# A softmax that streams from HBM: tiles of twelve rows in four slots, with an inner loop over groups of four, in place of tiles of eight in six slots

## The chip, the cores and the metric

The kernel runs on one core of one Trainium2 chip. The metric is the device time of one execution in microseconds (us); less is better. Times of before are those of nine runs, and one more execution was recorded by the hardware profiler.

## The reference

`x` has 32 x 512 rows of 1024 float32 numbers; `temperature` is 0.5. Each row gets a softmax of its own:

```python
scaled = x / temperature
shifted = scaled - np.max(scaled, axis=-1, keepdims=True)
exp_x = np.exp(shifted)
return exp_x / np.sum(exp_x, axis=-1, keepdims=True)
```

So 67.1 MB are read and 67.1 MB written. Nothing is shared between rows.

## The kernel before

The 16384 rows are cut into 16 tiles. A tile is 1024 rows: each of the 128 partitions holds 8 rows that follow each other in memory, 32 KB per partition, 4 MB per tile. The tile lies in one of six slots of the buffer `ring` (line 38); everything is done in place, and a slot goes from load to computation to store and then to the load of the tile six further on.

Each engine runs its own program, and semaphores set the order:

- **SyncE (SP)** issues all loads in order (lines 67 to 70). From tile 6 on it waits before each until the store that used the slot has landed (line 69). Last of all it issues the store of the last tile (lines 126 and 127) and waits for all stores.
- **TensorE** only turns "loaded" of each slot into a count, `ready` (line 72).
- **VectorE (DVE)** loops over the tiles (line 80). It waits for `ready` (line 82). Then, for three groups of 4, 2 and 2 rows: the maximum of each row (line 84), a wait for that result, and -2 times the maximum as a bias (line 91). Then, for the same groups: a wait until ScalarE has the sums, the reciprocal (line 96), a wait for it, and one multiplication per row (line 102). The helper `take` (line 63) waits for a semaphore and takes the count off again.
- **ScalarE (ACT)** loops over the tiles (line 109), and for each of the 8 rows computes exp(2x + bias) and its sum in one activation (line 115); ahead of rows 0, 4 and 6 it waits for the bias of that group.
- **GpSimd (POOL)** issues the stores of all tiles but the last, in order (lines 75 to 78). It waits once for the third load, and then before each store until VectorE has scaled the tile (line 77).

The groups are written out in Python, so VectorE's and ScalarE's programs hold one tile's instructions, and only the loop over tiles turns on the chip. Within it a row's place in `ring` is worked out in registers from the tile's number.

Of the kernel before, what the change touches and what calls it, by code (L numbers as in the profile page):

```python
# [1 line left out]

# [4 lines left out]

SLOTS, ROWS = 6, 8  # L10

GROUPS = [4, 2, 2]


@with_exitstack
def kernel(
    ctx: ExitStack,
    tc: tile.TileContext,
    x: bass.AP,
    temperature: bass.AP,  # L20
    out: bass.AP,
):
    nc = tc.nc
    f32 = mybir.dt.float32
    scale = 1.0 / float(temperature)
    extreme = mybir.AluOpType.max if scale > 0 else mybir.AluOpType.min

    P = 128
    xf = x.flatten_outer_dims()
    of = out.flatten_outer_dims()  # L30
    n, d = xf.shape
    tiles = n // (P * ROWS)
    assert tiles * P * ROWS == n and sum(GROUPS) == ROWS
    groups = [(sum(GROUPS[:g]), k) for g, k in enumerate(GROUPS)]
    of_group = dict(groups)

    pool = ctx.enter_context(tc.tile_pool(name="data", bufs=1))
    ring = pool.tile([P, SLOTS * ROWS, d], f32, name="ring")
    top = pool.tile([P, ROWS], f32, name="top")
    bias = pool.tile([P, ROWS], f32, name="bias")  # L40
    sums = pool.tile([P, ROWS], f32, name="sums")
    recip = pool.tile([P, ROWS], f32, name="recip")
    warm = pool.tile([P, 1], f32, name="warm")

    loaded = [tc.alloc_semaphore(f"loaded{s}") for s in range(SLOTS)]
    stored = [tc.alloc_semaphore(f"stored{s}") for s in range(SLOTS)]
    ready, topped, biased, summed, inverted, scaled, finished = (
        tc.alloc_semaphore(name)  # L50
        for name in ("ready", "topped", "biased", "summed", "inverted", "scaled", "finished")
    )

    def dram(t, i):
        return t[P * ROWS * i : P * ROWS * (i + 1), :].rearrange("(p k) d -> p k d", p=P, k=ROWS)

    def slot(i):
        s = i % SLOTS
        return ring[:, ROWS * s : ROWS * (s + 1), :]

    def take(engine, sem, count=1):

        engine.wait_ge(sem, count).then_inc(sem, -count)  # L63

    with tc.tile_critical(no_gpsimd_drain=True):  # L65

        for i in range(tiles):
            if i >= SLOTS:
                nc.sync.wait_ge(stored[i % SLOTS], 16 * (i // SLOTS))
            nc.sync.dma_start(out=slot(i), in_=dram(xf, i)).then_inc(loaded[i % SLOTS], 16)  # L70
        for i in range(tiles):
            nc.tensor.wait_ge(loaded[i % SLOTS], 16 * (i // SLOTS + 1)).then_inc(ready, 1)


        nc.gpsimd.wait_ge(loaded[2], 16)
        for i in range(tiles - 1):
            nc.gpsimd.wait_ge(scaled, len(groups) * (i + 1))
            nc.gpsimd.dma_start(out=dram(of, i), in_=slot(i)).then_inc(stored[i % SLOTS], 16)  # L78

        with nc.vector.Fori(0, tiles) as t:  # L80
            first = t % SLOTS * ROWS
            take(nc.vector, ready)
            for a, k in groups:
                nc.vector.tensor_reduce(  # L84
                    out=top[:, a : a + k],
                    in_=ring[:, bass.ds(first + a, k), :],
                    axis=mybir.AxisListType.X,
                    op=extreme,
                ).then_inc(topped, 1)
                take(nc.vector, topped)  # L90
                nc.vector.tensor_scalar_mul(  # L91
                    bias[:, a : a + k], in0=top[:, a : a + k], scalar1=-scale
                ).then_inc(biased, k)
            for a, k in groups:
                take(nc.vector, summed, k)
                nc.vector.reciprocal(  # L96
                    recip[:, a : a + k], sums[:, a : a + k]
                ).then_inc(inverted, 1)
                take(nc.vector, inverted)
                for b in range(a, a + k):  # L100
                    row = ring[:, bass.ds(first + b, 1), :]
                    ins = nc.vector.tensor_scalar_mul(row, in0=row, scalar1=recip[:, b : b + 1])  # L102
                ins.then_inc(scaled, 1)


        nc.scalar.activation(  # L106
            warm, nc.const_aps.tensor(0.0, (P, 1)), mybir.ActivationFunctionType.Exp
        )
        with nc.scalar.Fori(0, tiles) as t:
            first = t % SLOTS * ROWS  # L110
            for b in range(ROWS):
                row = ring[:, bass.ds(first + b, 1), :]
                if b in of_group:
                    take(nc.scalar, biased, of_group[b])
                nc.scalar.activation(  # L115
                    row,
                    row,
                    mybir.ActivationFunctionType.Exp,
                    bias=bias[:, b : b + 1],
                    scale=scale,  # L120
                    accum_out=sums[:, b : b + 1],
                ).then_inc(summed, 1)


        i = tiles - 1
        nc.sync.wait_ge(scaled, len(groups) * tiles)
        nc.sync.dma_start(out=dram(of, i), in_=slot(i)).then_inc(finished, 16)
        for i in range(tiles - SLOTS, tiles - 1):
            nc.sync.wait_ge(stored[i % SLOTS], 16 * (i // SLOTS + 1))
    with tc.tile_critical(no_gpsimd_drain=True):  # L130
        nc.sync.wait_ge(finished, 16, synchronizes=[nc.sync.lower_ap(slot(tiles - 1))])


# [1 line left out]
_INS = ['x', 'temperature']  # L135
_OUTS = [((32, 512, 1024), 'float32')]

_NUMBERS = {'temperature': 0.5}


# [26 lines left out]
```

## Time and profile before

| | |
|---|---|
| median of 9 runs | 318.43 us (318.25 to 319.11) |
| the profiled execution | 318.38 us, its span 316.6 us |
| VectorE busy | 244.4 us, 77% |
| ScalarE busy | 148.1 us, 47% |
| GpSimd busy | 8.3 us, 3% |
| bytes read, written | 67.11 MB, 67.11 MB: 424 GB/s over the span |
| reduce of 4 rows, of 2 rows (line 84) | 4416 ns, 2286 ns |
| multiplication of a row (line 102) | 749 ns |
| reciprocal of 4 values, of 2 (line 96) | 178 ns, 157 ns |
| activation of a row (line 115) | 1135 ns, 128 of them |
| loads (line 70), median from issue to landing | 49.4 us |
| stores (line 78), the same | 43.7 us |
| last store (line 127) | 17.2 us |

The span runs from the first to the last instruction of the profiled execution. Busy time leaves out what an engine's sequencer does for itself: register operations, branches and semaphores. In rows of tenths, each digit is the busy share of one fortieth of the span. A line of a timeline has the start, the duration, engine, source line, operation, what it writes and reads; in brackets is the idle time ahead of it and what ended it. DVEq and ACTq are the sequencers of VectorE and ScalarE, SPq that of SyncE.

### The profile page before, as it was taken

To read this page: it belongs to the slowest core of one execution; us is meant where nothing else is said; L and a number is where in the kernel's file an instruction comes from. 1 tells how busy PE (TensorE), PEld (TensorE's weight loads), DVE (VectorE), ACT (ScalarE), POOL (GpSimd) and SP (SyncE) were. 2 spreads that over 40 slices of the span, in tenths; PEclk is the share of its full clock that TensorE was granted. 3 is DMA by queue.
4 is the path that set the end of the run, shared out by engine and by line. 5 is a ranking of instruction groups with operands and counts; after the bars stand their busy time and mean duration, and the time that the engine had idled before them with its cause. 6 is when DMAs were issued, how large, how long until landed. Compare 5 with 4: busy or idle time off the path is not lost. (4 is left out here: it accounts for less than half of the span.)

```text
span 316.6 us, 1208 instructions
## 1 busy us (share of the span) xinstructions
DVE 244.4 (77%) x272; ACT 148.1 (47%) x258; POOL 8.3 (3%) x19
## 2 busy tenths in 40 slices
DVE  0299999999999999996959969597795978959600
ACT  1065655556464747380824709156190652907300
POOL 0000000000000000000000000000000000000000
DMA  8999999999999999999999999999999999999995
GB/s 319 410 460 402 397 455 406 464 397 464 402 460 418 443 439 422 447 414 455 406 460 402 460 418 447 422 439 443 418 451 410 460 397 464 402 460 418 443 431 236
DMA packets 4608, 134.22 MB, mean 424 GB/s; under 512 B 512, under 2 KB 512, under 8 KB 512
## 3 DMA queue, kind: packets, MB, share of 16 engines
q1 hardware_dynamic: 2448, 71.30, 52.6%
q0 software_dynamic: 2160, 62.92, 46.0%
HBM read 67.11 MB, written 67.11 MB: 424 GB/s over the span
## 5 line engine op out<-in xcount | busy, mean ns | idle before, releaser
L115 ACT ACTIVATE ring<-ring,bias x128 | 145.1, 1135 | 147.0 <-ACTq L63 147.0
L84 DVE TENSOR_REDUCE top<-ring 128x2 f32 (+1 forms) x48 | 143.8, 2996 | 39.3 <-DVEq L63 39.3
L102 DVE TENSOR_SCALAR ring<-ring,recip x128 | 89.1, 749 | 7.2 <-DVEq L63 1.5
L115 ACT ACTIVATION_READ_ACCUMULATOR ring<-ring,bias 128x1 f32 x128 | 24.0, 187 | 0.0
L78 POOL DMA_DIRECT2D out_dram<-ring x15 | 8.1, 542 | 270.9 <-DVE ring L102 238.4
L91 DVE TENSOR_SCALAR bias<-top 128x2 f32<-128x2 f32 (+1 forms) x48 | 8.2, 170 | 7.2
L96 DVE RECIPROCAL recip<-sums 128x2 f32<-128x2 f32 (+1 forms) x48 | 7.9, 164 | 0.0
L106 ACT ACT_TABLE_LOAD x1 | 1.3, 1283 | 0.9 <-SPq L65 0.9
L106 ACT ACTIVATE warm<-const-float32-0.0 128x1 f32<-128x1 f32 x1 | 0.2, 203 | 0.0
L148 POOL MEMSET const-float32-0.0<- 128x1 f32 x1 | 0.1, 99 | 0.2 <-issue 0.2
L148 POOL MEMSET const-bfloat16-1.0<- 128x1 bf16 x1 | 0.1, 103 | 0.0
L148 POOL MEMSET const-float32-1.0<- 128x1 f32 x1 | 0.1, 99 | 0.0
L148 POOL MEMSET const-uint8-127<- 128x1 uint8 x1 | 0.1, 99 | 0.0
## 6 DMA issues: line engine op xcount, KB each, us to landing
ring<-in_x_dram SPq DMA_DIRECT2D x16, 4096.0 KB, 49.4
out_dram<-ring POOLq DMA_DIRECT2D x15, 4096.0 KB, 43.7
out_dram<-ring SPq DMA_DIRECT2D x1, 4096.0 KB, 17.2
```

Of the source, the lines that this page charges most:

```text
L78: nc.gpsimd.dma_start(out=dram(of, i), in_=slot(i)).then_inc(stored[i % SLOTS], 16)
L84: nc.vector.tensor_reduce(out=top[:, a : a + k], in_=ring[:, bass.ds(first + a, k), :], axis=mybir.AxisListType.X, op=extreme,).then_inc(t ...
L91: nc.vector.tensor_scalar_mul(bias[:, a : a + k], in0=top[:, a : a + k], scalar1=-scale).then_inc(biased, k)
L96: nc.vector.reciprocal(recip[:, a : a + k], sums[:, a : a + k]).then_inc(inverted, 1)
L102: ins = nc.vector.tensor_scalar_mul(row, in0=row, scalar1=recip[:, b : b + 1])
L106: nc.scalar.activation(warm, nc.const_aps.tensor(0.0, (P, 1)), mybir.ActivationFunctionType.Exp)
L115: nc.scalar.activation(row, row, mybir.ActivationFunctionType.Exp, bias=bias[:, b : b + 1], scale=scale, accum_out=sums[:, b : b + 1],).th ...
L148: nc = _bacc.Bacc("TRN2", target_bir_lowering=False, num_devices=1)
```

## The change

There are now ten tiles of twelve rows per partition (6 MB each) and a last one of eight, in four slots of twelve rows: the buffer has 48 rows per partition, as before. All groups have four rows, three in a tile and two in the last. VectorE and ScalarE no longer have the groups written out: an inner loop on the chip turns once per group, with a count that is worked out from the tile's number, so that it turns twice in the last tile. Rows, bias, sums and reciprocals are now addressed through registers that hold the group's number. The counts on the semaphores follow: one per group in place of one per row on `biased` and `summed`. The order of loads and stores, the engines that issue them and the gate on the third load are as they were.

```diff
-SLOTS, ROWS = 6, 8
+TILES = [12] * 10 + [8]
+SLOTS = 4
 
-GROUPS = [4, 2, 2]
+GROUP = 4
...
+    groups = [k // GROUP for k in TILES]
...
+    ring = pool.tile([P, SLOTS * most, d], f32, name="ring")
...
+        rows = t[P * sum(TILES[:i]) : P * sum(TILES[: i + 1]), :]
+        return rows.rearrange("(p k) d -> p k d", p=P, k=TILES[i])
...
+    def loop_groups(engine, t):
+
+        if groups[-1] == groups[0]:
+            return engine.Fori(0, groups[0])
+        short = t // (tiles - 1) * (groups[0] - groups[-1])
+        return engine.Fori(0, groups[0] - short)
...
         with nc.vector.Fori(0, tiles) as t:
-            first = t % SLOTS * ROWS
+            first = t % SLOTS * most
             take(nc.vector, ready)
-            for a, k in groups:
+            with loop_groups(nc.vector, t) as g:
+                group = bass.ds(g * GROUP, GROUP)
                 nc.vector.tensor_reduce(
-                    out=top[:, a : a + k],
-                    in_=ring[:, bass.ds(first + a, k), :],
+                    out=top[:, group],
+                    in_=ring[:, bass.ds(first + g * GROUP, GROUP), :],
...
-                ).then_inc(biased, k)
-            for a, k in groups:
-                take(nc.vector, summed, k)
...
+                ).then_inc(biased, 1)
+            with loop_groups(nc.vector, t) as g:
+                group = bass.ds(g * GROUP, GROUP)
+                take(nc.vector, summed)
+                nc.vector.reciprocal(recip[:, group], sums[:, group]).then_inc(inverted, 1)
                 take(nc.vector, inverted)
-                for b in range(a, a + k):
-                    row = ring[:, bass.ds(first + b, 1), :]
-                    ins = nc.vector.tensor_scalar_mul(row, in0=row, scalar1=recip[:, b : b + 1])
+                for b in range(GROUP):
+                    row = ring[:, bass.ds(first + g * GROUP + b, 1), :]
+                    ins = nc.vector.tensor_scalar_mul(
+                        row, in0=row, scalar1=recip[:, bass.ds(g * GROUP + b, 1)]
+                    )
                 ins.then_inc(scaled, 1)
...
-            for b in range(ROWS):
-                row = ring[:, bass.ds(first + b, 1), :]
-                if b in of_group:
-                    take(nc.scalar, biased, of_group[b])
-                nc.scalar.activation(
...
+            with loop_groups(nc.scalar, t) as g:
+                take(nc.scalar, biased)
+                for b in range(GROUP):
+                    row = ring[:, bass.ds(first + g * GROUP + b, 1), :]
+                    column = bass.ds(g * GROUP + b, 1)
+                    ins = nc.scalar.activation(
...
+                ins.then_inc(summed, 1)
```

More of the change, by code (lines that the diff above doesn't have):

```diff
@@ L31 @@
     n, d = xf.shape
[L32 to L35, printed above, removed]
+    tiles, most = len(TILES), max(TILES)
+    assert sum(TILES) * P == n and all(k % GROUP == 0 for k in TILES)
+    groups = [k // GROUP for k in TILES]
+    assert all(g == groups[0] for g in groups[:-1]) and groups[-1] <= groups[0]
     pool = ctx.enter_context(tc.tile_pool(name="data", bufs=1))
[L38 to L42, printed above, removed]
+    ring = pool.tile([P, SLOTS * most, d], f32, name="ring")
+    top = pool.tile([P, most], f32, name="top")
+    bias = pool.tile([P, most], f32, name="bias")
+    sums = pool.tile([P, most], f32, name="sums")
+    recip = pool.tile([P, most], f32, name="recip")
     warm = pool.tile([P, 1], f32, name="warm")
@@ L54, in dram @@
     def dram(t, i):
-        return t[P * ROWS * i : P * ROWS * (i + 1), :].rearrange("(p k) d -> p k d", p=P, k=ROWS)
+        rows = t[P * sum(TILES[:i]) : P * sum(TILES[: i + 1]), :]
+        return rows.rearrange("(p k) d -> p k d", p=P, k=TILES[i])
     def slot(i):
-        s = i % SLOTS
-        return ring[:, ROWS * s : ROWS * (s + 1), :]
+        first = most * (i % SLOTS)
+        return ring[:, first : first + TILES[i], :]
     def take(engine, sem, count=1):
         engine.wait_ge(sem, count).then_inc(sem, -count)
+    def loop_groups(engine, t):
[3 more added lines that the diff above has]
+        return engine.Fori(0, groups[0] - short)
     with tc.tile_critical(no_gpsimd_drain=True):
@@ L76 @@
         for i in range(tiles - 1):
-            nc.gpsimd.wait_ge(scaled, len(groups) * (i + 1))
+            nc.gpsimd.wait_ge(scaled, sum(groups[: i + 1]))
             nc.gpsimd.dma_start(out=dram(of, i), in_=slot(i)).then_inc(stored[i % SLOTS], 16)
         with nc.vector.Fori(0, tiles) as t:
-            first = t % SLOTS * ROWS
+            first = t % SLOTS * most
             take(nc.vector, ready)
-            for a, k in groups:
+            with loop_groups(nc.vector, t) as g:
+                group = bass.ds(g * GROUP, GROUP)
                 nc.vector.tensor_reduce(
-                    out=top[:, a : a + k],
-                    in_=ring[:, bass.ds(first + a, k), :],
+                    out=top[:, group],
+                    in_=ring[:, bass.ds(first + g * GROUP, GROUP), :],
                     axis=mybir.AxisListType.X,
@@ L91 @@
                 nc.vector.tensor_scalar_mul(
-                    bias[:, a : a + k], in0=top[:, a : a + k], scalar1=-scale
-                ).then_inc(biased, k)
-            for a, k in groups:
-                take(nc.vector, summed, k)
-                nc.vector.reciprocal(
-                    recip[:, a : a + k], sums[:, a : a + k]
-                ).then_inc(inverted, 1)
-                take(nc.vector, inverted)
-                for b in range(a, a + k):
-                    row = ring[:, bass.ds(first + b, 1), :]
-                    ins = nc.vector.tensor_scalar_mul(row, in0=row, scalar1=recip[:, b : b + 1])
+                    bias[:, group], in0=top[:, group], scalar1=-scale
+                ).then_inc(biased, 1)
[3 more added lines that the diff above has]
+                nc.vector.reciprocal(recip[:, group], sums[:, group]).then_inc(inverted, 1)
+                take(nc.vector, inverted)
+                for b in range(GROUP):
[3 more added lines that the diff above has]
+                    )
                 ins.then_inc(scaled, 1)
@@ L109 @@
         with nc.scalar.Fori(0, tiles) as t:
-            first = t % SLOTS * ROWS
-            for b in range(ROWS):
-                row = ring[:, bass.ds(first + b, 1), :]
-                if b in of_group:
-                    take(nc.scalar, biased, of_group[b])
-                nc.scalar.activation(
[L116 to L122, printed above, removed]
+            first = t % SLOTS * most
+            with loop_groups(nc.scalar, t) as g:
[4 more added lines that the diff above has]
+                    ins = nc.scalar.activation(
+                        row,
+                        row,
+                        mybir.ActivationFunctionType.Exp,
+                        bias=bias[:, column],
+                        scale=scale,
+                        accum_out=sums[:, column],
+                    )
+                ins.then_inc(summed, 1)
         i = tiles - 1
-        nc.sync.wait_ge(scaled, len(groups) * tiles)
+        nc.sync.wait_ge(scaled, sum(groups))
         nc.sync.dma_start(out=dram(of, i), in_=slot(i)).then_inc(finished, 16)
```

## The prediction

> **What bounds the kernel now.** I read the page's busy rows first, then the table of stretches, then the store issues in order of time, then one stretch of VectorE.
>
> The page's rows of busy time (tenths in 40 slices):
>
> ```profile
> DVE 244.4 (77%) x272; ACT 148.1 (47%) x258; POOL 8.3 (3%) x19
> ...
> DVE  0299999999999999996959969597795978959600
> ...
> DMA  8999999999999999999999999999999999999995
> ...
> q1 hardware_dynamic: 2448, 71.30, 52.6%
> q0 software_dynamic: 2160, 62.92, 46.0%
> ```
>
> The table of stretches (us; DVE, ACT, POOL busy; clock; DMA share; GB/s):
>
> ```profile
> 33.00:126.00 93.00, 87.61 (x102) 54.98 (x96) 3.33 (x6) 1.00 1.01 431
> 126.00:280.00 154.00, 123.11 (x137) 73.31 (x128) 4.80 (x9) 1.00 1.00 433
> 280.00:298.00 18.00, 15.23 (x17) 9.16 (x16) 0.00 (x0) 1.00 1.00 433
> 298.00:312.80 14.80, 0.08 (x1) 0.00 (x0) 0.00 (x0) 1.00 0.99 430
> 312.80:316.60 3.80, 0.00 (x0) 0.00 (x0) 0.00 (x0) 1.00 0.02 9
> ```
>
> The 16 DMA engines are full from about 2 us to about 313 us: the two queues take 98.6% of 316.6, or 312.2 us. The bytes are the bound. There are 4608 packets, of which 512 are under 512 B; the other 4096 are one 32 KB run per partition and transfer, 256 on each engine. The packet records give 1.21 us each, whether loads run alone, stores alone, or both in turn, one packet from each queue. So a 4 MB transfer is 8 rounds, 9.7 us alone and 19.4 us beside the other queue.
>
> The store issues, start and duration (us):
>
> ```profile
> 110.79 0.53 POOL L78 DMA_DIRECT2D out_dram<-ring  x1 [15.58 <-DVE ring L102]
> 126.90 0.53 POOL L78 DMA_DIRECT2D out_dram<-ring  x1 [15.58 <-DVE ring L102]
> 143.44 0.53 POOL L78 DMA_DIRECT2D out_dram<-ring  x1 [16.01 <-DVE ring L102]
> 162.82 0.53 POOL L78 DMA_DIRECT2D out_dram<-ring  x1 [18.85 <-DVE ring L102]
> 182.17 0.53 POOL L78 DMA_DIRECT2D out_dram<-ring  x1 [18.81 <-DVE ring L102]
> ```
>
> Until about 127 us a tile leaves every 16.1 us: VectorE works off the tiles loaded at the start at its own speed. Then every 19.4 us, because VectorE has caught up and takes each tile as it lands. So VectorE has 3.3 us to spare per tile of 8 rows, and it is the one engine that could become the bound.
>
> VectorE in its compute-bound stretch, one tile's start and part of its end:
>
> ```profile
> 110.41 4.41 DVE L84 TENSOR_REDUCE top<-ring 128x4 f32 x1
> 114.97 0.17 DVE L91 TENSOR_SCALAR bias<-top 128x4 f32<-128x4 f32 x1
> 115.11 2.29 DVE L84 TENSOR_REDUCE top<-ring 128x2 f32 x1
> ...
> 120.27 0.18 DVE L96 RECIPROCAL recip<-sums 128x4 f32<-128x4 f32 x1
> 120.59 2.74 DVE L102 TENSOR_SCALAR ring<-ring,recip  x4
> 123.25 0.15 DVE L96 RECIPROCAL recip<-sums 128x2 f32<-128x2 f32 x1
> ```
>
> A group of four costs 115.11 - 110.41 = 4.70 us to reduce and 123.25 - 120.27 = 2.98 us to scale.
>
> **The change, part by part.**
>
> *Bytes.* 134.22 MB before and after. With 12 rows a partition's run is 48 KB, so I take a packet as 1.5 x 1.21 = 1.815 us. No row shows a 48 KB packet. The price per packet and transfer has a lower end: a 4 B semaphore packet took 9 ns, so if each data packet carries so much besides its bytes, 256 - 176 = 80 fewer packets an engine, and 10 fewer semaphore packets (32 transfers become 22), save at most 90 x 9 ns = 0.8 us. The upper end is every 48 KB run split in two: 10 x 2 transfers x 16 + 16 = 336 packets an engine, 80 more than now, +0.7 us. I take -0.4 us, the half of the first, since a long run has shown no reason to be split.
>
> The Trainium skill (DMA: Bandwidth & Descriptors, "Anatomy of one DMA") puts about 2.0 us of fixed cost on each DMA, so by it ten fewer would save 20 us if each were paid in turn. The trace disagrees: the first three loads ended at 12.98, 22.66 and 32.34 us, 9.68 us apart, which is eight packets and no gap; the fixed part is a latency that the next transfer covers. The same page ("Where 436 GB/s comes from") gives a ceiling of 435.2 GB/s; 134.22 MB at that takes 308.4 us, an estimate that leaves at most 3.8 us to save of 312.2.
>
> *VectorE, per tile of 12.* In the before form it would be 3 x 4.70 + 3 x 2.98 = 23.0 us. The inner loops add register and branch instructions. The built program has, between one bias and the next reduce, a register operation, a move, a subtraction, the branch and two register operations; before has one register operation. The sequencer's records at the outer loop's turn before give prices: addition at 93.13, branch 93.20, move 93.39, semaphore 93.48, long register operation 93.57 (125 ns; short ones 69). So about 0.07, 0.19, 0.09, 0.10 and 0.2 us between starts. Between bias and reduce: 0.07 + 0.07 + 0.07 + 0.19 + 0.2 + 0.1 = 0.7 against 0.1 us, and an addition ahead of the bias 0.07: about +0.68 us a group, exposed, since the reduce cannot be issued earlier: 3 x 0.68 = 2.0 us. In the scale loop the long register operation stands between reciprocal and first multiply: +0.14 us a group, 0.4 us; the rest is issued while four multiplies (2.74 us) run. Leaving the first loop for the second costs +0.2. Sum: 23.0 + 2.6 = **25.7 us** (from 23.0, all hidden, to 26.9, the additions half as long again). Per tile the DMA needs 16 x 1.815 = 29.0 us, so VectorE stays ahead in the middle.
>
> *ScalarE.* 12 rows x 1.13 = 13.6 us, beginning about 5 us into a tile; its loop turns hide under a running activation (before, the first turn's addition, branch and move stood at 23.98 to 24.20, under the activation from 23.25 to 24.38). Its third group ends near 20.3 us, the scale loop wants it at 22.7. Nothing.
>
> *Last tile, two groups of four.* Reduces 2 x 5.38 = 10.8; the second bias releases ScalarE at about 10.2, four rows end at 14.9; scale ends at 15.0 + 3.2 = 18.2 us. Before: 281.87 to 298.08, 16.2 us.
>
> *The schedule.* The first reduce before came at 13.70 = 4.0 + 9.7; after, 4.0 + 14.5 = 18.5. The store gate (third load) before at 4.0 + 29.0 = 33.0, as the trace has it; after at 4.0 + 43.6 = 47.6, which costs nothing, since four loads (58 us of DMA) are queued: the engines only read longer and write later. Load 3 and store 0 then share, store 0 ends near 76.7, and load 4 starts. Store 1 is issued at 18.5 + 2 x 25.7 = 69.9; the first store before took 4.25 us from issue to first packet, so 74.2, in time with 2 us to spare. From there a load lands every 29.0 us: load 4 at 107.5, load 9 at 252.7, and load 10 (8 rounds of 1.815 + 1.21 us) at 276.9. VectorE: 18.5 + 9 x 25.7 = 249.8, so it has caught up and starts tile 9 at 253.1, tile 10 at 278.8, ending at 297.0. Before, the last data packets ended at 313.7 (one engine 314.8), and the last store needs 9.7 us alone: its packets must be there by 304, so its issue by about 301 (before it took 3.4 us from issue to first packet). **Slack: 4 us.** The floor holds.
>
> *Sum against the profiled execution.* 318.38 us was measured with a span of 316.6 (1.8 around it); 318.38 - 0.4 = **318.0**. The median of the runs, 318.43, is 0.05 above that execution: no difference.
>
> **The rivals.**
>
> *A, the floor holds (0.65).* 317.4 to 318.6, around 318.0. For it: share 1.00 in every stretch, and 4 us of slack at the only place where the queues can run dry.
>
> *B, VectorE becomes the bound (0.20): slower.* The chain is first landing + ten tiles + the last: 18.5 + 10c + 18.2 must stay under 301, so c under 26.4 us. That is 0.7 us over my 25.7, or 0.23 us a group, a quarter of what I priced from other instructions. Beyond it every 0.1 us of c, paid by ten tiles, costs 1 us, and the DMA engines stand idle ahead of the last two stores. At c = 26.9 it is 18.5 + 269 + 18.8 + 3.4 + 9.7 = 319.4 of data end against 313.7, about 324 us. Against it: the branch and moves have rows in this trace.
>
> *C, a gap at a hand-over, or a slower long packet (0.08): slower.* Four slots hold the same 48 rows but hand back in larger pieces; where store 0 ends at 76.7 and store 1 is late, or the two ends stand dry, 1 to 2 us are lost, and a split run costs up to 0.7: 319 to 320.5.
>
> *D, the packet saving is larger (0.07).* One engine ends 1.1 us after the others before, its store packets being a little longer (1.23 to 1.25 us); a third fewer may take that too: 0.8 + 0.4, 317.2.
>
> **How the numbers follow.** This measurement can tell about 0.2%, 0.64 us, from no change: faster is under 317.8, slower over 319.1. Of A's 0.65 I give 0.17 to faster, 0.43 to within, 0.05 to slower; B is slower; of C 0.06 slower and 0.02 within; D is faster. Together 0.24 faster, 0.45 within, 0.31 slower. Forecast 318.0. The range reaches from D, 317.2, to where B has used over half of its chance, 322.5; for the likeliest case alone 317.4 to 318.6.
>
> **What would show it.** DMA share 1.00 from 2 to 313 us; 3168 packets; reduce to reduce 5.4 us, reciprocal to reciprocal 3.1 us, a tile 25.7 us in the early stretch; first reduce at 18.5, first store issue at 47.6; last reduce starting near 279 and the last store issued near 297; store issues 29 us apart late. Wrong if a tile takes over 26.4 us, if the DMA row falls under 9 anywhere before the last slice, or if 48 KB packets are not 1.5 times 32 KB ones.

## The result, and the profile after

The changed kernel takes 319.56 us (median of 9 runs, 319.19 to 319.99) against 318.43 us: ratio 1.0033, 95% interval 1.0025 to 1.0042. It is slower by 1.1 us. The forecast was 318.0, a little faster than before. The profiled execution took 319.65 us with a span of 317.8.

The page of the changed kernel, rows of busy time and queues:

```profile
DVE 237.6 (75%) x224; ACT 149.9 (47%) x258; POOL 5.7 (2%) x14
...
DVE  0057898788879879878887887978887877798600
...
DMA  7999999999999999999999999999999999999994
...
DMA packets 3168, 134.22 MB, mean 422 GB/s; under 512 B 352, under 2 KB 352, under 8 KB 352
...
q1 hardware_dynamic: 1728, 71.30, 52.5%
q0 software_dynamic: 1440, 62.92, 45.8%
```

The DMA engines are as full as before and the packets are the 3168 that were counted: no 48 KB run was split. Only the ends differ: 7 in place of 8 at the start, 4 in place of 5 at the end. The table of stretches of the changed kernel, and then the same two last stretches of the kernel before:

```profile
126.00:280.00 154.00, 128.88 (x121) 83.46 (x144) 2.67 (x5) 1.00 1.00 432
280.00:298.00 18.00, 15.35 (x15) 8.16 (x15) 0.53 (x1) 1.00 0.99 429
298.00:313.00 15.00, 2.92 (x5) 1.11 (x2) 0.00 (x0) 1.00 1.00 426
313.00:317.80 4.80, 0.00 (x0) 0.00 (x0) 0.00 (x0) 1.00 0.08 34
```

```profile
298.00:313.00 15.00, 0.08 (x1) 0.00 (x0) 0.00 (x0) 1.00 0.98 424
313.00:316.60 3.60, 0.00 (x0) 0.00 (x0) 0.00 (x0) 1.00 0.02 9
```

The new time is in the last row. After 313 us the kernel before has a share of 0.02 in 3.60 us; the changed one has 0.08 in 4.80 us, which is 6 us of one DMA engine (0.08 x 4.80 x 16): a few engines still work when the others are done. The row above it reads 1.00 all the same: a mean over 16 engines hides the last one.

VectorE in a tile of the changed kernel (start, duration):

```profile
77.62 4.42 DVE L95 TENSOR_REDUCE top<-ring  x1 [0.73 <-issue]
82.28 0.17 DVE L102 TENSOR_SCALAR bias<-top  x1 [0.23 <-DVEq L66]
83.17 4.42 DVE L95 TENSOR_REDUCE top<-ring  x1 [0.72 <-issue]
...
88.58 0.18 DVE L108 RECIPROCAL recip<-sums  x1 [0.60 <-DVEq L66]
89.18 2.74 DVE L112 TENSOR_SCALAR ring<-ring,recip  x4 [0.41 <-DVEq L66]
91.83 0.17 DVE L108 RECIPROCAL recip<-sums  x1
```

Reduce to reduce is 83.17 - 77.62 = 5.55 us (4.70 before), reciprocal to reciprocal 91.83 - 88.58 = 3.25 (2.98). The bracket "issue" is time in which the engine waited for nothing that the profile shows; the records of VectorE's sequencer put its register operations and the branch there. A tile can be read from the store issues:

```profile
203.62 0.53 POOL L88 DMA_DIRECT2D out_dram<-ring  x1 [25.70 <-DVE ring L112]
229.85 0.53 POOL L88 DMA_DIRECT2D out_dram<-ring  x1 [25.70 <-DVE ring L112]
256.11 0.53 POOL L88 DMA_DIRECT2D out_dram<-ring  x1 [25.72 <-DVE ring L112]
284.06 0.53 POOL L88 DMA_DIRECT2D out_dram<-ring  x1 [27.42 <-DVE ring L112]
```

The first three are 26.23 and 26.26 us apart, against the DMA's 29.0. VectorE catches up with the loads only for tile 9, whose load lands from 254.18 (first DMA engine) to 256.7 (last). The start of that tile, and then the last store, by SyncE, of the changed kernel and of the kernel before:

```profile
257.42 4.42 DVE L95 TENSOR_REDUCE top<-ring  x1 [1.61 <-DVEq L66]
302.74 0.35 SPq L141 DMA_DIRECT2D out_dram<-ring  x1
```

```profile
298.11 0.35 SPq L127 DMA_DIRECT2D out_dram<-ring  x1
```

Where the 1.2 us between the two traces come from shows in the landings. Each transfer raises its semaphore once per DMA engine, so the trace has 16 landing times for each. This table is worked out from them, for all kernels of this study. Its columns: how far the 16 are apart in the second load transfer; how far the last is behind the first in a store transfer late in the run (the last whose first landing is before 295 us, but one that still has other work behind it); and the first and last landing of the last store.

```
kernel                     median us  ratio    load 1   store near 290  last store
before                     318.43     -        0.59     1.52            313.69  315.31
after                      319.56     1.0033   1.52     2.88            313.69  316.55
e1  loops, 8 rows          327.62     1.0287   0.42     1.97            324.33  324.49
e2  written out, 12 rows   319.52     1.0030   1.28     1.63            313.46  315.17
e3  12 rows, 16 KB         320.88     1.0073   1.01     2.65            315.01  317.90
e4  12 rows, stores by SP  321.09     1.0076   1.70     5.35            313.46  318.78
e5  12 rows as 8 + 4       319.69     1.0044   0.80     2.34            314.03  316.60
e6  the same, 48 KB apart  320.16     1.0059   0.88     2.58            314.12  316.93
e7  8 rows, 96 KB apart    318.48     1.0002   0.68     1.75            313.69  315.53
e8  8 rows, 16 KB          319.78     1.0045   0.44     1.48            315.15  316.79
e9  after, first load cut  318.90     1.0019   1.18     2.51            313.84  316.10
e10 e2, first load cut     318.43     1.0009   1.05     2.10            313.37  315.57
e11 8 rows, long start     318.61     1.0006   0.48     2.17            313.52  315.71
e12 e2 again               318.29     1.0003   1.15     1.93            313.28  315.20
e13 after again            319.54     1.0030   0.87     2.82            313.64  316.52
e14 e2 again, beside e13   319.04     1.0026   0.89     2.46            313.55  315.98
e15 last tile written out  318.87     1.0019   0.86     2.10            313.34  315.58
e16 e2, last store late    319.83     1.0036   1.55     3.25            314.67  316.85
e17 before, last store late 318.60    1.0008   0.60     1.48            313.73  315.35
e18 before, still later    321.52     1.0087   0.68     1.34            318.28  318.43
```

The landings are those of the traced execution. In e2 it was the fastest of the runs (318.27 us) and in e4 the slowest (321.85); in the others it lies within 0.3 us of the median.

Before and after, the first DMA engine ends at 313.69 in both. The last one ends at 315.31 and 316.55. The difference of the two traces is in how far the last engine is behind the first, and it was 1.36 us further behind already near 290 us, before the last store was issued. The engines between them are later too: the mean of the 16 landings of the last store is 313.96 before and 314.33 after.

### The profile page after: what moved, and what is told of

Its sections match the earlier page's. It is cut to its first block, busy times and chain, and to the rows that moved or that the text cites. A ratio compares the mean times of both kernels' runs of the same rounds, so it can differ in the third digit from the quotient of the medians.

```text
span 317.8 us, 1878 instructions
## 1 busy us (share of the span) xinstructions
DVE 237.6 (75%) x224; ACT 149.9 (47%) x258; POOL 5.7 (2%) x14
## 2 busy tenths in 40 slices
DMA packets 3168, 134.22 MB, mean 422 GB/s; under 512 B 352, under 2 KB 352, under 8 KB 352
## 5 line engine op out<-in xcount | busy, mean ns | idle before, releaser
L95 DVE TENSOR_REDUCE top<-ring x32 | 141.3, 4417 | 36.4 <-DVEq L66 21.2
L112 DVE TENSOR_SCALAR ring<-ring,recip x128 | 87.7, 749 | 13.2 <-DVEq L66 13.2
L128 ACT ACTIVATION_READ_ACCUMULATOR ring<-ring,bias x128 | 23.9, 187 | 0.0
L108 DVE RECIPROCAL recip<-sums x32 | 5.5, 173 | 8.0 <-DVEq L66 8.0
L102 DVE TENSOR_SCALAR bias<-top x32 | 5.5, 171 | 7.4 <-DVEq L66 7.4
L88 POOL DMA_DIRECT2D out_dram<-ring x10 | 5.5, 546 | 278.7 <-DVE ring L112 230.9
## 6 DMA issues: line engine op xcount, KB each, us to landing
ring<-in_x_dram SPq DMA_DIRECT2D x10, 6144.0 KB, 36.6
```

Of the source, the lines that this page charges most:

```text
L95: nc.vector.tensor_reduce(out=top[:, group], in_=ring[:, bass.ds(first + g * GROUP, GROUP), :], axis=mybir.AxisListType.X, op=extreme,).th ...
L102: nc.vector.tensor_scalar_mul(bias[:, group], in0=top[:, group], scalar1=-scale).then_inc(biased, 1)
L108: nc.vector.reciprocal(recip[:, group], sums[:, group]).then_inc(inverted, 1)
L128: ins = nc.scalar.activation(row, row, mybir.ActivationFunctionType.Exp, bias=bias[:, column], scale=scale, accum_out=sums[:, column],)
```

## The experiments

Each edit is against the kernel named. Theories changed on the way; each expectation says which it weighs. Single traces are one execution each, while the medians are of 5 to 12 runs.

**e1: inner loops over groups of four, at tiles of eight.** The changed kernel with the tiles and slots of before:

```diff
-TILES = [12] * 10 + [8]
-SLOTS = 4
+TILES = [8] * 16
+SLOTS = 6
```

> Inner loops alone: sixteen tiles of eight rows in six slots, as before, with the inner loops over groups of four. Theory skew (what ends last is one DMA engine that runs behind the others, and the long packets put it further behind; VectorE is not the bound): packets are those of before, so 318.4 us, ratio 0.999 to 1.001. Theory VectorE (the loops make a tile long, the last store is issued late, and DMA engines run dry ahead of it): the loops add 2 x 0.85 + 2 x 0.25 us to a tile of 8 rows, less one group's own costs, so a last store about 1.5 to 2 us later than 298.1, and some of it in the time: 318.8 to 320.

Measured: 327.62 us, 1.0287 (1.0273 to 1.0301). Both expectations were far too low. The stretches near the end and two store issues:

```profile
296.00:306.00 10.00, 8.20 (x6) 5.50 (x9) 0.00 (x0) 1.00 0.98 419
306.00:314.00 8.00, 5.36 (x9) 3.77 (x8) 0.00 (x0) 1.00 0.00 0
314.00:325.80 11.80, 0.00 (x0) 0.00 (x0) 0.00 (x0) 1.00 0.83 355
```

```profile
276.22 0.53 POOL L88 DMA_DIRECT2D out_dram<-ring  x1 [18.20 <-DVE ring L112]
294.94 0.53 POOL L88 DMA_DIRECT2D out_dram<-ring  x1 [18.19 <-DVE ring L112]
```

A tile takes 18.72 us on VectorE, so sixteen end at 13.75 + 16 x 18.72 = 313.3, where the last store is issued; from 306 to 314 the DMA share is 0.00. This is the rival in which VectorE becomes the bound, at tiles of eight. With two groups of four, VectorE also waits 1.6 us in each tile for ScalarE's second group. The last tile of e2 (below), eight rows in two groups of four without a loop, has the same wait. One line of e1, then three of e2:

```profile
310.04 0.18 DVE L108 RECIPROCAL recip<-sums  x1 [1.59 <-DVEq L66]
```

```profile
280.19 4.42 DVE L95 TENSOR_REDUCE top<-ring 128x4 f32<-128x4096 f32 x1 [1.03 <-DVEq L66]
294.47 0.18 DVE L108 RECIPROCAL recip<-sums 128x4 f32<-128x4 f32 x1 [1.57 <-DVEq L66]
297.57 0.35 SPq L147 DMA_DIRECT2D out_dram<-ring  x1
```

That tile lasts 17.4 us, against 16.2 for the last tile of the kernel before with its groups of 4, 2 and 2. So about half of the 2.6 us that a tile is longer in e1 belongs to the groups of four, not to the loops, and no run has the loops with the old groups. The groups alone would, by an estimate, not have made the last store late: 281.87, where the last tile began before, and 17.4 give 299.3.

In the tiles of twelve rows that wait is gone and a row costs 26.23 / 12 = 2.19 us in place of 18.72 / 8 = 2.34. So the two halves of the change are not two small things: the loops over groups of four cost 9.1 us at tiles of eight, and the larger tiles hide nearly all of it.

**e2, e12, e14: larger tiles alone.** The changed kernel, groups of four included, with the groups written out in Python, for VectorE and ScalarE, the last tile behind the loop:

```diff
-            with loop_groups(nc.vector, t) as g:
+            for g in range(n):
...
+        with nc.vector.Fori(0, tiles - 1) as t:
+            vector_tile(t, groups[0])
+        vector_tile(tiles - 1, groups[-1])
```

> Tiles alone: ten tiles of twelve rows and one of eight in four slots, the groups of four written out, so that a tile takes about 23.1 us on VectorE in place of 26.2. Theory skew: 319.3 to 319.8 us, as the changed kernel, ratio 1.003. Theory VectorE: last store issued some 5 us earlier than 302.7, and the time back at 318.0 to 318.5.

> The kernel with twelve rows and groups written out, once more for a second trace: its first one was of its fastest run. Theory first packet: 319.4 us, loads land 1.3 to 1.7 us apart at the start and the last engine ends that and a drift of about 1 us behind. Theory drift: the loads start as in the first trace and the lag grows by more than 1.5 us.

> The same tiles with the groups written out, on the same chip: last store issued near 297.7 us. Theory late store (what the loops cost is that the last store comes when the DMA engines have no other packets, so that its first packet is not covered by one before it): 0.5 to 0.9 us under the changed kernel. Theory spread (the difference lies in how far apart the DMA engines start and drift, which the engines' loops do not touch): the same as the changed kernel within 0.2 us.

Measured: 319.52 (1.0017 to 1.0042), 318.29 (0.9993 to 1.0013) and 319.04 (1.0013 to 1.0039), on three occasions, each on another chip, and from 317.96 to 320.81 between runs. The last store is issued near 298 us each time. So the larger tiles alone cost nothing on one occasion and up to 1.0 us on another. Their first engine ends at 313.28 to 313.55, 0.1 to 0.4 us before that of the kernel before. That fits the saving of the packets that the prediction put at 0.4; the last engine's lag takes it back.

**e3, e8: the length of packets.** All transfers in pieces of four rows, 16 KB packets; e3 from the changed kernel, e8 from the kernel before:

```diff
-            nc.sync.dma_start(out=slot(i), in_=dram(xf, i)).then_inc(loaded[i % SLOTS], 16)
+            for g in range(groups[i]):
+                nc.sync.dma_start(out=part(slot(i), g), in_=part(dram(xf, i), g)).then_inc(
+                    loaded[i % SLOTS], 16
+                )
...
```

> The changed kernel with each transfer cut into pieces of four rows, so that a packet is 16 KB in place of 48 KB (three times as many transfers and packets, the same tiles, slots and loops). Theory skew, if the length of a packet is what matters: the first packets cost 0.6 us or more less, the lagging engine is less behind, 318.0 to 318.9 us; if it goes by bytes or by transfers, 319.5 or more. Theory VectorE: 319.5, since no engine's work changes.

> The kernel before with each transfer cut into two of four rows: 16 KB packets, partitions 32 KB apart as before, 512 data packets an engine in place of 256. At 4.3 ns for each of the 256 more, +1.1 us: 319.5 us. Theory distance: first loads land within 0.6 us. Theory length: the engines start no further apart than before, so the same.

Measured: 320.88 (1.0060 to 1.0087) and 319.78 us (1.0032 to 1.0059). Already the first engine ends later in both (315.01 and 315.15 against 313.69). In e8 an engine has 256 more data packets and 32 more semaphore packets for 1.4 us more time, some 5 ns each, which is the price that shorter packets have here. The lag of the last engine hardly shrank in e3: 2.65 us, against 2.88 and 2.82 in the two traces of the changed kernel. So it does not need packets of 48 KB.

**e4: no stores by GpSimd.** SyncE issues all transfers, in an order that was written out, without the gate on the third load:

```diff
-        nc.gpsimd.wait_ge(loaded[2], 16)
-        for i in range(tiles - 1):
-            nc.gpsimd.wait_ge(scaled, sum(groups[: i + 1]))
-            nc.gpsimd.dma_start(out=dram(of, i), in_=slot(i)).then_inc(stored[i % SLOTS], 16)
+        for i in range(tiles - 1):
+            store(i)
+            if i >= LEAD and i - LEAD + SLOTS < tiles:
+                load(i - LEAD + SLOTS)
...
```

> The changed kernel with all stores issued by SyncE on the queue of the loads (a load follows one store behind the one that frees its slot), none by GpSimd. Theory skew, if the lag belongs to the packets of GpSimd's queue: no engine over 1 us behind at the end, 317.5 to 318.5 us; if it belongs to the DMA engine, 319.5. Theory VectorE: 319.5 or more, since the work of VectorE is the same and loads come later.

Measured: 321.09 us (1.0062 to 1.0090), and the queue line shows that all went one way:

```profile
q1 hardware_dynamic: 3168, 134.22, 97.8%
```

The first engine ends at 313.46, so the queue as a whole does not run dry, but four engines fall behind by over 3 us, the last by 5.35. The Trainium skill (DMA: Bandwidth & Descriptors, "Latency and other measured facts") says that engines 7 and 15 are usually slower and, as a best guess, ties this to the descriptor rings of transfers issued from GpSimd. One engine or more falls behind in every kernel here that was not idle at its end. Between 60 and 285 us the packets that took 6 to 90 ns over the median add up to 1.9 us in the changed kernel and to 1.8 us in e4, which has no such transfers; and e4 has 27 packets that took over 90 ns longer, up to 1.3 us, where the changed kernel has 3. So this case speaks against that tie as the only cause. Which engines they are the trace does not say.

**e5, e6, e7: the distance between partitions.** e5 moves a tile of twelve as two blocks of memory of eight and four rows; e6 makes the same cut but leaves the partitions 48 KB apart; e7 is the kernel before with partitions 96 KB apart:

```diff
-        rows = t[P * sum(TILES[:i]) : P * sum(TILES[: i + 1]), :]
-        return rows.rearrange("(p k) d -> p k d", p=P, k=TILES[i])
+        return [
+            t[start + P * lo : start + P * hi, :].rearrange("(p k) d -> p k d", p=P, k=hi - lo)
+            for lo, hi in cut[TILES[i]]
+        ]
...
```

> The changed kernel, each tile of twelve rows moved as two transfers, eight rows and four, each over memory of its own: 32 KB and 16 KB packets, and partitions that lie 32 KB and 16 KB apart in memory in place of 48 KB (336 data packets an engine in place of 176, which at 4.3 ns each, from the cut into 16 KB, cost 0.7 us). Theory distance (the engines start apart, and one falls behind, because partitions lie 48 KB apart): first loads land within 0.6 us of each other on the 16 engines, and the time is 318.8 to 319.4 us. Theory length (it goes with the length of packets): the same as the next kernel.

> The same cut into eight rows and four, so the same packets and transfers as the kernel before this one, but partitions stay 48 KB apart in memory. Theory distance: first loads land 1 to 1.6 us apart, 320.0 to 320.5 us. Theory length: the same as the kernel before this one, within 0.3 us.

> The kernel before with one thing changed: three tiles that follow each other share a stretch of memory, so that partitions lie 96 KB apart in place of 32 KB (three times 32 KB, no power of two); packets, transfers, slots and engines' work as before. Theory distance: first loads land 1 us or more apart, 319.2 to 319.8 us. Theory length: 318.4 us, first loads within 0.6 us.

Measured: 319.69, 320.16 and 318.48 us (1.0002, 0.9993 to 1.0011). e7 refutes the plain form of the theory: 96 KB is as good as 32. e5 and e6 start almost equally far apart (0.80 and 0.88), and both are over 2.3 us apart near 290 us. e6 is 0.5 us slower than e5, with no run in common (319.67 to 319.84 against 319.96 to 320.53); that is the direction of the theory, but e5 stayed above the 318.8 to 319.4 it gave. What the 0.5 us are is not shown.

**e9, e10, e11: the first packet.** e9 and e10 cut the first load into 32 KB and 16 KB packets (e9 in the changed kernel, e10 in the written-out one); e11 gives the kernel before a 48 KB first packet.

```diff
-            nc.sync.dma_start(out=slot(i), in_=dram(xf, i)).then_inc(loaded[i % SLOTS], 16)
+            for lo, hi in [(0, 8), (8, 12)] if i == 0 else [(0, TILES[i])]:
+                nc.sync.dma_start(
+                    out=slot(i)[:, lo:hi, :], in_=dram(xf, i)[:, lo:hi, :]
+                ).then_inc(loaded[i % SLOTS], 16)
...
```

> The changed kernel with its first load alone cut into eight rows and four, so that the first packet of each DMA engine is 32 KB in place of 48 KB; everything else as it was (eight more packets an engine). Theory first packet (how far apart the 16 engines start goes with the length of their first packet, stays to the end, and the last engine sets the time): first loads land 0.6 to 0.9 us apart in place of 1.5, and the time is 318.7 to 319.1 us. Theory drift (the last engine loses its time along the way): 319.4 to 319.7.

> The same cut of the first load, with the groups of four written out. Theory first packet: 318.2 to 318.9 us, and less spread between runs than the same kernel without the cut. Theory drift: 319.5.

> The opposite: the kernel before with a long first packet. Tiles 0 and 1 share a stretch of memory, the first load takes twelve rows of it (48 KB packets) and the second the other four. All else as before; tile 0 begins 5 us later, which VectorE has to spare. Theory first packet: loads land 1.3 to 1.7 us apart in place of 0.6, and the time is 319.0 to 319.6 us. Theory drift: 318.4.

Measured: 318.90 (1.0010 to 1.0028), 318.43 (0.9992 to 1.0026) and 318.61 (0.9997 to 1.0014). e9 landed where the theory put it, but not for its reason: its loads are still 1.18 us apart. The runs of e10 spread no less than those of e12 (317.82 to 320.25). And e11, with the long first packet, starts only 0.48 us apart and is not slower. The theory falls.

**e13, e15, e16: the late last store.** On one chip, with e14: the changed kernel again; the same with its last tile written out, so that the last store comes earlier; and the written-out kernel with one unused reduce in the last tile, so that it comes later.

```diff
+                if n < groups[0] and g == 1:
+                    nc.vector.tensor_reduce(
+                        out=spare,
+                        in_=ring[:, bass.ds(first + a, GROUP), :],
+                        axis=mybir.AxisListType.X,
+                        op=extreme,
+                    )
```

> The changed kernel itself, beside the next three on one chip. Both theories: 319.0 to 319.7 us, last store issued near 302.7 us, and the first packets of that store long on the DMA engines that had run out of other packets.

> The changed kernel with its inner loops in the first ten tiles, and the last tile alone written out, so that its last store is issued about 2 us earlier (near 300.8) and tiles of twelve rows take 26.2 us as in the changed kernel. Theory late store: 0.4 us or more under the changed kernel, near the kernel with all groups written out. Theory spread: the same as the changed kernel.

> The kernel with the groups written out, and in the last tile a second reduce of its second group, whose result nothing uses, so that the last store is issued 4.6 us later, near 302.3, as in the changed kernel. Theory late store: 0.5 to 0.9 us over the kernel without it, near the changed kernel. Theory spread: the same as the kernel without it.

Last store issued at 302.64, 298.54 (e14), 299.58 and 303.75 us; medians 319.54, 319.04, 318.87 and 319.83. The two with the early store are 0.5 to 1.0 us under the two with the late one, though not in order among themselves. But the landings say that this is at most partly its doing. For the last engine, from the store near 290 us to the end it is 24.42 us in both traces of the changed kernel, 24.30 in e15, 24.16 in e14 and 24.15 in e16, the latest of all. In these traces the last engine of e13 ends 0.94 us after that of e15, and that of e16 0.87 after that of e14; 0.8 to 0.9 us of it were there already at the store near 290 us.

**e17, e18: the late store in the kernel before.** One and two unused reduces of four rows between the last scaling and the last store, which waits for them:

```diff
...
-        nc.sync.wait_ge(scaled, len(groups) * tiles)
+        nc.sync.wait_ge(passed, 1)
```

> The kernel before, with one reduce of four rows (4.4 us) on VectorE between the last scaling and the last store, its result unused, so that the last store is issued near 302.7 us, as in the changed kernel, in place of 298.1; tiles, packets and all other work as before. Theory late store: store 14 ends alone near 303.7, the last store's first packet comes at about that time and is partly exposed: 318.8 to 319.4 us. Theory spread: 318.4, as before.

> The same with two such reduces (8.8 us): last store near 307.1 us, after the other packets have ended. Theory late store: the DMA engines stand idle from about 303.7 to 308, so 4 to 5.5 us over before: 322.5 to 324. Theory spread: also slower, since nothing is left to move, but by no more than the idle time; the step from one reduce to two tells where the cover ends.

Measured: 318.60 (1.0008, 0.9999 to 1.0017) with the store issued at 302.70, and 321.52 (1.0087) with 307.33. The stretches of e17 and then of e18:

```profile
298.00:302.00 4.00, 3.97 (x2) 0.00 (x0) 0.00 (x0) 1.00 1.00 434
302.00:306.00 4.00, 0.67 (x1) 0.00 (x0) 0.00 (x0) 1.00 0.96 369
306.00:313.00 7.00, 0.00 (x0) 0.00 (x0) 0.00 (x0) 1.00 1.02 440
```

```profile
298.00:302.00 4.00, 3.97 (x2) 0.00 (x0) 0.00 (x0) 1.00 0.99 426
302.00:306.00 4.00, 4.00 (x2) 0.00 (x0) 0.00 (x0) 1.00 0.44 188
306.00:313.00 7.00, 1.30 (x1) 0.00 (x0) 0.00 (x0) 1.00 0.70 300
```

In e17 the first packet of the last store took 0.2 to 1.0 us longer than 1.21 on 13 engines: the rate in the row from 302 falls to 369 GB/s at a share of 0.96. That they had just run out of other packets is the likely reason, but an idle engine alone is not enough: in e18, where all 16 were idle, these first packets took 1.21 to 1.22 us. The last engine, 1.5 us behind, still had packets to cover the wait, and it sets the time. So 4.6 us of delay cost about 0.1 us, within the interval of no change, and the next 4.6 us cost 2.9. The slack of the prediction was real. It ends between the two, near 304.4 if from there every microsecond counts (307.33 - 2.92, an estimate).

## Why the prediction was wrong, point by point

- **What bounds the kernel**: right. The DMA share is 0.98 to 1.00 in every stretch between 126 and 313 us in both kernels.
- **The packets**: right. 48 KB packets took 1.815 us at the median, as put; none was split. At their median durations, and with each beginning 3 to 4 ns before the one ahead of it ends, the packets of an engine take 309.80 us before and 309.37 after, so the 0.4 us are there; that the prediction's choice, half of a bound, hit them was luck. The 2.0 us that the prediction takes from the Trainium skill (DMA: Bandwidth & Descriptors, "Anatomy of one DMA") are the page's figure for transfers issued by GpSimd, while the three loads held against it are SyncE's. GpSimd's stores agree with those loads: when no load is left, two first land 9.68 us apart (284.66 and 294.34 in the trace of before).
- **VectorE's tile**: 26.23 us against 25.7, and the last store at 302.74 against 297.0. The terms were too small because the register operations that recompute row addresses last 257 and 220 ns here, where the long one before had 125. Tile 9 also began later (257.42 against 253.1): its load landed from 254.18 on in place of 252.7, because load 4, put to start at 76.7, was issued at 77.48 and moved its first packet at 81.66; and VectorE starts a tile when the last of 16 engines has landed, here 2.6 us after the first. So the slack of 4 us was gone: the last store came 1.7 us after the 301 that the prediction allowed. By these traces the last engine paid at most some 0.3 us for that (24.42 us from the store near 290 us to the end, against 24.15 to 24.30).
- **"The floor holds"**: it did not. The step "Before, the last data packets ended at 313.7 (one engine 314.8)" took that one engine's lag as given, and the sum, 318.38 - 0.4, carried the saving in the packets' usual durations over to the last engine, with nothing for packets that take longer. This is the step that failed. The lag grew by 1.24 us (1.62 to 2.86 at the end), and the time is that of the last landing: 315.31 goes with 318.38, 316.55 with 319.65. The last rival even expected the lag to shrink with fewer packets. The mean engine did not gain either. What packets took over their median comes to 1.49 us an engine before and 2.32 after: 1.40 and 1.86 in the first 60 us, in which both queues begin, 0.09 and 0.17 from there to 300 us, and 0.00 and 0.29 in the late last store. That is 0.83 us more, twice the saving.
- **The rival with VectorE as the bound**: it did not decide here, but at tiles of eight it costs 9.1 us (e1). The threshold, a last store at about 301, was a little strict: at 302.7 the cost is about 0.1 us, at 307.3 it is 3.0 (e17, e18).

What stays open is why the lag is larger. The kernels with tiles of eight, not idle at the end, are 1.5 to 2.2 us apart near 290 us; those with twelve 1.6 to 3.3, and 5.35 in e4. With eight one engine stands out: the one next to last is 0.4 to 0.7 us behind the first. With twelve that one is 0.5 to 3.0 behind in the kernels with GpSimd's stores. All with twelve start further apart (0.80 to 1.70 against 0.42 to 0.68).

Refuted as its single cause are the length of packets (e3), GpSimd's queue (e4), the distance of partitions (e7) and the length of the first packet (e11). Not tested is the number of slots: every kernel with twelve rows has four, every one with eight has six. With four, fewer loads are queued: a load takes 36.6 us at the median from issue to landing, of which 29.0 are its own transfer beside the stores, and in the kernel before 49.4, of which 19.4. In the changed kernel no load packet starts from 69.9 to 81.7 us. Between 60 and 285 us six of the seven kernels with eight rows have no packet over 90 ns longer than the median (e18 has 21), and all with twelve but e5 have 3 to 27, mostly in loads. Whether slots or rows do this no run tells.

The inner loops may add to it: 12-row kernels with them had 2.1 to 2.9 (e4 left out), those without 1.6 to 3.3, which overlap, so one trace each does not tell. Nor is it shown how much of the 1.1 us each half of the change gives: on one chip the changed kernel was 0.5 us over the written-out one, on another occasion the written-out one was as slow as it. No version here beats the kernel before beyond its interval.

## What to carry to other kernels

A kernel that keeps all DMA engines full ends with the last of 16, so a prediction to a few tenths of a per cent needs the spread of their landings, not the mean share, which reads 1.00 in both cases. An inner loop on the chip costs about 0.85 us per turn here where each turn waits for its own result. It is hidden only while the whole chain, from the first landing over all tiles to the last store, ends before the other packets do: in e1 a tile on VectorE (18.72 us) took less than its two transfers (19.4), and the time still rose by 9.1 us. A late last store costs almost nothing until the other packets run out, and then most of its delay (e17, e18).

## What the runs showed of the hardware that was not expected

The sixteen engines start 0.4 to 1.7 us apart, and the last is 1.3 to 5.4 us behind the first near 290 us. Only where all had run out of packets ahead of the last store do they end together, 0.16 us apart (e1, e18). In the kernel before, the packets between 60 and 285 us that took longer than the median are 6 to 43 ns longer, four fifths of that time in GpSimd's stores, 1.1 us in all; with loads and stores in one queue (e4) single packets take up to 1.3 us longer and four engines drift, by up to 5.35. A taken branch on VectorE is followed by the next instruction 0.19 us after its start (82.58 to 82.77 in the changed kernel), one that falls through 0.08 us (88.12 to 88.20). The Trainium skill (Advanced Engine Details and Errata, "Control Flow Timing") gives about 108 ns for a compare-and-branch, which lies between the two.
